# Four loads and one sum moved in a two-block transformer kernel

## The chip, the cores and the metric

The kernel runs on one core of a Trainium2 chip. The metric is device time in microseconds (us) of one launch. Three runs of the kernel before gave 2931.91, 2932.08 and 2934.31 us, a median of 2932.08 us.

## The reference

Two transformer blocks, one after the other, on 1024 tokens of width 1024, all in float32. What the change touches:

```
# block 1
u = rmsnorm(x);  z = u @ w_in;  q, k, v, pz, ga, gp = split(z)
for g in 3 head groups (dilations 1, 4, 16):
    s = q_g k_g^T / 8 + alibi_g          # bias by distance, -1e30 outside the window
    o_g, lse_g = softmax(s) v_g
a = sum over g of softmax(lse)_g * o_g
p = pool branch of pz
merged = sigmoid(u @ w_ga) * (a @ w_att_out) + sigmoid(u @ w_gp) * (p @ w_pool_out)
h = x + merged @ w_out
m = rmsnorm(h)
h = h + relu(m @ w_mlp_in)^2 @ w_mlp_out          # first feed-forward
# block 2: other attention, a recurrent unit, the same gates, and
h = h + relu(rmsnorm(h) @ w_ff1)^2 @ w_ff2        # second feed-forward
return rmsnorm(h)
```

## The kernel before

All matrices are held with channels on the 128 partitions and tokens along the free dimension; a tile `z` is 128 x 1024 float32. Every float32 product is made of three products of rounded parts (`hi*hi`, `hi*lo`, `lo*hi`), so each weight and each operand is split: ScalarE copies it to `hi`, VectorE subtracts to get `lo` (`hilo`, L476; weights in `split`, L323). A dense job (`dense`, L430) makes one 128 x 1024 result: for each of up to eight 128-row pieces of the weight it issues six matmuls of 128 x 512, and then calls `tick`.

**Order of the work.** The program is a list of jobs written in order; the schedule is the order in which instructions are issued, engine by engine, and every engine's queue is first in, first out. All data loads and stores go through SyncE's (SP's) queue. Before a job runs, the weights of the next jobs are split and those after them loaded (`run`, L390). Work that is not dense (attention steps, the merging of attention groups, sums of weights) is kept in generators in three lanes; `tick` adds the job's rate to a credit, and for every whole credit `advance` (L289) runs each lane by one step. So a step stands in the queues behind a given matmul. Buffers come from pools; a tile of a pool can be written once the last instruction that used its buffer is done, and the instruction that writes it waits in its queue for that. Pool `pz` has 36 buffers for nearly all 128 x 1024 tiles; a phase (`phase`, L269) opens a small pool of its own with five more (`t4`) and closes that of the phase before.

**Attention of block 1.** For each group, `vfn` (L1874) computes v (`v_job`, L661). For groups 1 and 2 v is stored to DRAM and read back in another order (`vd`, L705). Then `attn1` (L717) is put into lane 0. Its first step takes a buffer for the bias `alibi` and issues its load (L720 and L721); its second step issues the scores of step 0 on TensorE (L738), its third the softmax (L753 on VectorE adds the bias from SBUF to the scores in PSUM and takes the minimum of the negative; L758 on ScalarE takes exp). Later steps transpose (L768), copy (L770, L771), and multiply by v (L784). Meanwhile jobs of the pool branch run on TensorE.

**End of attention.** `combine1` (L815) merges the groups. Beside it the eight `pool_out_job` (L937) compute, copy to `po` and store it to DRAM. `att_end` (L952) drains the lanes, opens phase phC, and loads the first three chunks of the normed input (`u_load`, L959, tiles `uraw` of the phase's `t4`) from DRAM, where they were stored early in the kernel. Then `att_out_job(m)` (L963), m = 0 to 7, loads chunk m + 3, splits chunk m into `ub` on ScalarE and VectorE, issues 12 matmuls, and ScalarE copies the PSUM tile to `merged` (L976). PSUM has two tiles for such jobs.

**Feed-forward, second half.** `w_mlp_out` and `w_ff2` are applied by seven block products instead of eight (Strassen-like) over four blocks b of the hidden width. For each product i in the order 1, 2, 3, 6, 7, 5, 4 (`SEVEN_OUT`) there are four steps p, one per pair of output chunks: 12 matmuls in `seven` (L1125) into one of four PSUM banks, then `prep_step` splits the operand of the next product on steps p = 0 and p = 2 (`out_prep`, L1200: `obh`, `obl`), then the result is added (`out_ev`, L1267) to the residual `h` (`c11`, `c12`, `c21`, `c22` are its halves) and to a running sum `u` (tile `uu`). In the first block b = 0, the steps of product 1 also load the residual: step p issues two loads of 512 KB from DRAM (L1017, called at L1239) before its matmuls. For product 1 ScalarE copies the bank to `u` (L1276) and VectorE adds the bank to `c11` (L1278); product 2 adds to `c11` again by L1278. Both feed-forwards run this code.

Of the kernel before, what the change touches and what calls it, by code (L numbers as in the profile page):

```python
# [13 lines left out]
ALU = mybir.AluOpType  # L14
# [4 lines left out]
NC = D // P  # L19
# [177 lines left out]
class Kern:  # L197
# [519 lines left out]
    def attn1(self, g, src):  # L717
        nc = self.nc
        d = DIL[g]
        bias = self.z(nm="alibi")  # L720
        nc.sync.dma_start(bias, self.ins["alibi"][g])  # L721
        steps = []
        for j in range(8):
            prev = (j > 0) if g == 0 else (j % 2 == 1 if g == 1 else False)
            for hp in range(2):
                steps.append((j, hp, prev))
        n = len(steps)
        ot = {}

        def scores(t):  # L730
            j, hp, prev = steps[t]
            w = (2 if prev else 1) * P
            q, k = src["q", hp], src["k", hp]
            pss = []
            for h in range(2):
                sl = slice(64 * h, 64 * h + 64)
                ps = self.bank()
                nc.tensor.matmul(  # L738
                    ps[:, :w], q[sl, j * P:(j + 1) * P], k[sl, (j + 1) * P - w:(j + 1) * P], start=True, stop=True)
                pss.append(ps)  # L740
            return pss

        def softmax(t, pss):
            j, hp, prev = steps[t]
            w = (2 if prev else 1) * P
            if hp == 0:
                ot[j] = self.ph.tile([P, 4, 66], F32, tag="o", name="o", bufs=3)
            o = ot[j]
            s = p = self.ph.tile([P, 512], F32, tag="s", name="s", bufs=3)
            for h in range(2):  # L750
                hh = 2 * hp + h
                b1 = (hh + 1) * 256
                nc.vector.tensor_tensor_reduce(  # L753
                    out=s[:, h * w:(h + 1) * w], in0=pss[h][:, :w], in1=bias[:, b1 - w:b1],
                    scale=-1.0, scalar=BIG, op0=ALU.add, op1=ALU.min, accum_out=o[:, hh, 64:65])
            for h in range(2):
                hh = 2 * hp + h
                nc.scalar.activation(  # L758
                    p[:, h * w:(h + 1) * w], s[:, h * w:(h + 1) * w], AF.Exp,
                    bias=o[:, hh, 64:65], scale=-1.0, accum_out=o[:, hh, 65:66])  # L760
            return p

        def flip(t, p):
            nb = 2 if steps[t][2] else 1
            w = nb * P
            ps = self.bank()
            for q in range(2 * nb):
                nc.tensor.transpose(ps[:, q * P:(q + 1) * P], p[:, q * P:(q + 1) * P], self.ident())  # L768
            pt = self.ph.tile([P, 512], F32, tag="pt", name="pt", bufs=3)
            nc.scalar.activation(pt[:, :w], ps[:, :w], AF.Copy)  # L770
            nc.vector.tensor_copy(pt[:, w:2 * w], ps[:, w:2 * w])  # L771
            return pt

        def values(t, pt):
            j, hp, prev = steps[t]
            nb = 2 if prev else 1
            o = ot[j]
            ps = self.bank()
            for h in range(2):
                hh = 2 * hp + h  # L780
                for b in range(nb):
                    kt = j - nb + 1 + b
                    v0 = (kt % 4) * 256 + 64 * hh
                    nc.tensor.matmul(  # L784
                        ps[:, 64 * h:64 * h + 64], pt[:, (h * nb + b) * P:(h * nb + b + 1) * P],
                        src["v", kt // 4][:, v0:v0 + 64], start=(b == 0), stop=(b == nb - 1))
            nc.vector.tensor_copy(
                o[:, 2 * hp:2 * hp + 2, 0:64], ps[:, :P].rearrange("p (h e) -> p h e", h=2))
            if hp == 1:
                scr = self.oscr[g]  # L790
                if d == 1:
                    dst = scr[j * P:(j + 1) * P, :]
                elif d == 4:
                    dst = scr.rearrange("(i d) c -> d i c", d=4)[j // 2, (j % 2) * P:(j % 2 + 1) * P]
                else:
                    dst = scr.rearrange("(i d) c -> d i c", d=8)[j]
                nc.sync.dma_start(dst, ot.pop(j).rearrange("p h e -> p (h e)"))

        yield
        pss = scores(0)  # L800
        yield
        p, pt = {}, {}
        for t in range(n + 2):
            if t < n:
                p[t] = softmax(t, pss)
                yield
            if 0 <= t - 1 < n:
                pt[t - 1] = flip(t - 1, p.pop(t - 1))
            if t >= 2:
                values(t - 2, pt.pop(t - 2))  # L810
            if t + 1 < n:
                pss = scores(t + 1)
            yield
# [123 lines left out]
    def pool_out_job(self, un, m):  # L937
        nc = self.nc

        def fn():  # L940
            ps = self.lin(un, 0, self.pms)
            t = self.z(nm="po")
            nc.scalar.activation(t, ps, AF.Copy)
            nc.sync.dma_start(self.po[m], t)
            if m == NC - 1:
                self.pms = [None] * 6
        return fn
# [4 lines left out]
    def att_end(self):  # L952
        self.drain()
        self.phase("phC")
        self.uraw = {}
        for c in range(3):
            self.u_load(c)

    def u_load(self, c):  # L959
        self.uraw[c] = self.t4(nm="uraw")  # L960
        self.nc.sync.dma_start(self.uraw[c], self.ud[c])

    def att_out_job(self, ua, m):  # L963
# [300 lines left out]
            self.uu[p // 2] = self.z(nm="uu")  # L1264
        return self.uu[p // 2][:, (p % 2) * H:(p % 2) * H + H]

    def out_ev(self, after=None):  # L1267

        nc = self.nc
        V, G = nc.vector, nc.gpsimd  # L1270

        def ev(i, p, ps):
            u = self.half_u(i, p)
            c11, c12, c21, c22 = (half(self.h[2 * p + e], a) for e in range(2) for a in range(2))
            if i == 1:
                nc.scalar.activation(u, ps, AF.Copy)  # L1276
            if i in (1, 2):
                V.tensor_tensor(c11, ps, c11, ALU.add)  # L1278
            elif i == 3:
                V.tensor_tensor(c12, ps, c12, ALU.add)  # L1280
            elif i == 6:
                V.tensor_tensor(u, ps, u, ALU.add)  # L1282
                G.tensor_tensor(c12, c12, u, ALU.add)  # L1283
            elif i == 7:
                V.tensor_tensor(u, ps, u, ALU.add)
                G.tensor_tensor(c22, c22, u, ALU.add)
                G.tensor_tensor(c21, c21, u, ALU.add)
            elif i == 5:
                V.tensor_tensor(c12, ps, c12, ALU.add)
                V.tensor_tensor(c22, ps, c22, ALU.add)  # L1290
            else:
                V.tensor_tensor(c21, ps, c21, ALU.add)
            if after:
                after(i, p)
        return ev

    def ff(self, pr, w1, w2, gname, after):
        pr.rate = 1.0
        for i in range(N_IN0):
            un = Unit(w1, 0, NC, i * P, P)  # L1300
            pr.job([un], self.ff_in_job(un, i), 4 if i == N_IN0 - 1 else None)
        steps = []
# [15 lines left out]
        for n, i in order:  # L1318
            quad, st = pairs[n]
            extra = before_out(tail[i]) if n == nq - 1 and i in tail else None  # L1320
            un = Oper(quad, i)
# [6 lines left out]
        for b in range(N_BLK):  # L1328
            two = twos(b)
            for i in SEVEN_OUT:  # L1330
                for p in range(4):
                    un = two[i, p // 2]
                    steps.append(((un, None)[p % 2], self.block_step(Pick(un, p % 2), b, p, self.out_ev())))
        end = after == self.end_after
        for n, (un, fn) in enumerate(steps):
            ahead = 6 if end and n >= len(steps) - 4 else 4 if isinstance(un, Oper) else 3
# [7 lines left out]
        for i in SEVEN_OUT:  # L1344
            for p in range(4):
                un = two[i, p // 2]
# [494 lines left out]
    def program(self):  # L1841
# [17 lines left out]
        for g in range(3):  # L1859
# [8 lines left out]
            for c in range(2):  # L1868
                un = Unit("w_in", 0, NC, 768 + 256 * g + P * c, P)
# [4 lines left out]
            def vfn(vf=vf, g=g):  # L1874
                if g == 0:
                    self.rcols()
                    self.phase("phA")
                vf()
                self.bg[0].append(self.attn1(g, qkv[g]))
                if g == 2:  # L1880
                    self.bg[0].append(self.combine1())
# [6 lines left out]
        for half in (1, 0):  # L1888
            un = Unit("grp", 7 * half, 7, 0, P)
            pr.job([un], self.grp_job(un, half))  # L1890
        for m in range(NC):
            un = Unit("w_pool_out", 0, 6, P * m, P)
# [3 lines left out]
        for m in range(NC):  # L1896
            un = Unit("w_att_out", 0, 2, P * m, P)
            pr.job([un], self.att_out_job(un, m), 2)
        pr.job([], lambda: (self.bg[2].append(self.weight_sums(N_SUMS)), self.bg[1].append(self.lru_const())))
        for m in range(NC):  # L1900
            un = Unit("w_in", 0, NC, 3072 + P * m, P)
            pr.job([un], self.ga_job(un, m))
            un = Unit("w_in", 0, NC, 4096 + P * m, P)
            pr.job([un], self.gp_job(un, m))
        for m in range(NC):
            un = Unit("w_out", 0, NC, P * m, P)
# [41 lines left out]
        for hh in range(2):  # L1948
            pr.rate = 1.0 if hh == 0 else 1.2
            for c in range(2):  # L1950
                un = Unit("w_in_2", 0, NC, 256 * hh + P * c, P)
                pr.job([un], self.qk2_job(un, qkv2[hh], ("q", c), 0.125, 2 * hh + c))
            for c in range(2):
                un = Unit("w_in_2", 0, NC, 512 + 256 * hh + P * c, P)
# [32 lines left out]
        for m in range(NC):  # L1987
            if m == NC - 1:
                pr.job([], self.lru_end, 0)
            un = Unit("w_att_o", 0, 4, P * m, P)  # L1990
# [3 lines left out]
        for m in range(NC):  # L1994
            un = Unit("w_rec_o", 0, NC, P * m, P)
            pr.job([un], self.rec_job(un, m))
        for m in range(NC):
            un = Unit("w_out_2", 0, NC, P * m, P)
# [210 lines left out]
```

## Time and profile before

| | |
|---|---|
| median of three runs | 2932.08 us |
| the profiled execution, whole | 2933.28 us |
| its span, first to last instruction | 2931.5 us |
| TensorE busy | 2860.9 us (98%) |
| VectorE, ScalarE, GpSimd busy | 1918.1, 1166.6, 935.3 us |
| mean granted TensorE clock | 0.989 |

The 1.8 us between the profiled execution and its span lie outside the first and the last instruction. TensorE is busy nearly always, so the few stretches in which it stands, or runs at a lower granted clock (1.00 is full speed), are where the other engines and the loads show in the time. In a row of the timeline the first number is the start, the second the duration, and the bracket at the end is how long the engine had been idle and what ended that.

### The profile page before, as it was taken

Reading aid. Unit: us, or ns where it says so; the run is one execution under the profiler, and the core shown is the slowest. Engines: PE = TensorE matmul, PEld = TensorE weight load, DVE = VectorE, ACT = ScalarE, POOL = GpSimd, SP = SyncE. Lnnn points to the kernel's source line nnn. Section 1 sums busy time; section 2 is a strip of 40 time slices with the busy share of each in tenths; the row PEclk is TensorE's granted clock in tenths of the full one; section 3 lists DMA queues with packets and bytes.
Section 4 is the critical chain, followed back from the end, with each engine's and each line's share of the span. In section 5 each row is a group of like instructions: output and inputs, shape, how many; then the busy total and the mean of one; then the engine's idle time right before and its main releaser. Section 6 shows DMA issues by size and latency. Waiting matters only on the chain. (4 is left out here: it accounts for less than half of the span.)

```text
span 2931.5 us, 35187 instructions
## 1 busy us (share of the span) xinstructions
PE 2860.9 (98%) x13422; PEld 2353.4 (80%) x13422; DVE 1918.1 (65%) x2441; ACT 1166.6 (40%) x1762; POOL 935.3 (32%) x482
## 2 busy tenths in 40 slices
PE   9999999999999999999999999999999899999997
PEld 8888877888878878887878778788888788878886
DVE  6434456666765558888744336999655855569897
ACT  3322234223344444334333325565424354444344
POOL 0021102554144423334500005555144144413336
PEclk9999999999999999999999999999999999999999
DMA  4221136677233354442233222121776232264452
GB/s 162 79 69 51 69 114 221 257 275 267 80 108 115 115 212 155 157 152 86 89 122 92 95 72 69 61 79 69 281 299 223 83 118 103 106 222 158 152 167 85
DMA packets 136599, 402.34 MB, mean 137 GB/s; under 512 B 13808, under 2 KB 32368, under 8 KB 136432
## 3 DMA queue, kind: packets, MB, share of 16 engines
q1 hardware_dynamic: 136432, 400.10, 39.0%
q8 instruction: 106, 1.74, 0.2%
q14 instruction: 61, 0.50, 0.0%
HBM read 287.75 MB, written 112.30 MB: 136 GB/s over the span
## 5 line engine op out<-in xcount | busy, mean ns | idle before, releaser
L1132 PE MATMUL bk<-obl,whi 128*128 128x512 f32 x864 | 338.4, 392 | 8.6 <-DVE obl L478 8.6
L477 ACT ACTIVATE whi<-raw 128x512 fp32r<-128x512 f32 (+2 forms) x256 | 204.9, 808 | 348.3 <-PE bk L1132 234.4
L1132 PE MATMUL bk<-obh,whi 128*128 128x512 f32 x864 | 338.0, 391 | 1.6 <-DVE h L1290 1.6
L1132 PE MATMUL bk<-obh,wlo 128*128 128x512 f32 x864 | 337.8, 391 | 0.3 <-DVE wlo L478 0.3
L439 PE MATMUL mm<-uh,whi 128*128 128x512 f32 x896 | 288.0, 403 | 5.2 <-ACT uh L490 2.5
L439 PE MATMUL mm<-ul,whi 128*128 128x512 f32 x896 | 279.1, 393 | 0.3 <-DVE ul L491 0.3
L439 PE MATMUL mm<-uh,wlo 128*128 128x512 f32 x896 | 278.5, 392 | 0.3 <-DVE wlo L339 0.3
L478 DVE TENSOR_TENSOR wlo<-raw,whi 128x512 fp32r<-128x512 f32 (+2 forms) x256 | 254.5, 997 | 36.5 <-ACT whi L477 36.4
L1132 PE MATMUL bk<-tt,whi 128*128 128x512 f32 x896 | 275.8, 389 | 0.0
L378 POOL TENSOR_TENSOR wsum<-wsum 128x1024 f32<-128x1024 f32 x64 | 182.6, 2863 | 230.7 <-DMA wsum<-in_w 228.4
L339 DVE TENSOR_TENSOR wlo<-raw,whi 128x1024 fp32r<-128x1024 f32 (+3 forms) x140 | 228.3, 1636 | 34.0 <-ACT whi L338 33.9
L439 PEld LDWEIGHTS mm<-uh,whi 128*128 128x128 f32 x896 | 163.3, 190 | 64.5 <-issue 27.5
L439 PEld LDWEIGHTS mm<-ul,whi 128*128 128x128 f32 x896 | 169.5, 189 | 37.8 <-DVE ul L491 1.5
L439 PEld LDWEIGHTS mm<-uh,wlo 128*128 128x128 f32 x896 | 169.1, 189 | 37.6 <-DVE wlo L339 1.1
L1132 PEld LDWEIGHTS bk<-obl,whi 128*128 128x128 f32 x864 | 163.3, 189 | 43.8 <-DVE obl L478 9.8
L1132 PEld LDWEIGHTS bk<-tt,whi 128*128 128x128 f32 x896 | 168.2, 188 | 34.8
L1283 POOL TENSOR_TENSOR h<-h,uu 128x512 f32<-128x512 f32 x32 | 70.9, 2228 | 386.4 <-DVE uu L1282 386.4
L1132 PEld LDWEIGHTS bk<-obh,whi 128*128 128x128 f32 x864 | 163.1, 189 | 36.5 <-DVE h L1290 2.0
L1132 PEld LDWEIGHTS bk<-obh,wlo 128*128 128x128 f32 x864 | 163.3, 189 | 34.5 <-DVE wlo L478 0.8
L338 ACT ACTIVATE whi<-raw 128x1024 fp32r<-128x1024 f32 (+3 forms) x140 | 135.6, 974 | 137.3 <-PE mm L676 52.5
L1132 PE MATMUL bk<-tt,wlo 128*128 128x512 f32 x448 | 174.3, 389 | 0.0
L478 DVE TENSOR_TENSOR obl<-hraw,obh 128x1024 fp32r<-128x1024 f32 x112 | 154.6, 1381 | 13.3 <-ACT obh L477 10.2
(355 smaller groups left out, 6212.3 us busy)
## 6 DMA issues: line engine op xcount, KB each, us to landing
raw<-in_w SPq DMA_DIRECT2D x190, 512.0 KB
wsum<-in_w SPq DMA_DIRECT2D x64, 512.0 KB
sums<-wsum SPq DMA_DIRECT2D x64, 512.0 KB
hraw<-hid SPq DMA_DIRECT2D x64, 512.0 KB
raw<-sums SPq DMA_DIRECT2D x64, 512.0 KB
hid<-h SPq DMA_DIRECT2D x56, 512.0 KB
wraw<-in_w SPq DMA_DIRECT2D x28, 512.0 KB
rb<-in_rpb SPq DMA_DIRECT2D x24, 384.0 KB
```

The lines of the kernel that those rows point to most:

```text
L338: nc.scalar.activation(un.hi, un.raw, AF.Copy)
L339: nc.vector.tensor_tensor(un.lo, un.raw, f32(un.hi), ALU.subtract)
L378: G.tensor_tensor(d, x, y, f)
L439: nc.tensor.matmul(dst[a], w, half(x, a), start=(i == 0 and q == 0), stop=(i == n - 1 and q == 2),)
L477: self.nc.scalar.activation(hi, src, AF.Copy)
L478: self.nc.vector.tensor_tensor(lo, src, f32(hi), ALU.subtract)
L1132: nc.tensor.matmul(ps, w[:, k * P:(k + 1) * P], x, start=(k == 0 and q == 0), stop=(k == n - 1 and q == 2))
L1283: G.tensor_tensor(c12, c12, u, ALU.add)
```

## The change

Three edits. The bias of each attention group is loaded in `vfn` before `vf()`, that is ahead of the group's v job, and `attn1` uses that tile. The first three input chunks are loaded by the jobs `pool_out_job` m = 5, 6 and 7, before their matmuls, and all eight `uraw` tiles come from pool `pz` instead of the phase's `t4`. In block b = 0 of each feed-forward's second half, product 1 is no longer added to `c11` on VectorE; it is only copied to `u`, and after product 2 has been added to `c11`, GpSimd adds `u` to it. The loads of the residual stay where they are.

```
     def attn1(self, g, src):
-        bias = self.z(nm="alibi")
-        nc.sync.dma_start(bias, self.ins["alibi"][g])
+        bias = self.alibi
...
     def pool_out_job(self, un, m):
         def fn():
+            if m == 0:
+                self.uraw = {}
+            if m >= NC - 3:
+                self.u_load(m + 3 - NC)
             ps = self.lin(un, 0, self.pms)
...
     def att_end(self):
         self.drain()
         self.phase("phC")
-        self.uraw = {}
-        for c in range(3):
-            self.u_load(c)
     def u_load(self, c):
-        self.uraw[c] = self.t4(nm="uraw")
+        self.uraw[c] = self.z(nm="uraw")
...
-    def out_ev(self, after=None):
+    def out_ev(self, after=None, first=False):
...
             if i == 1:
                 nc.scalar.activation(u, ps, AF.Copy)
-            if i in (1, 2):
+            if i == 1 and first:
+                pass
+            elif i in (1, 2):
                 V.tensor_tensor(c11, ps, c11, ALU.add)
+                if first:
+                    G.tensor_tensor(c11, c11, u, ALU.add)
...
-    steps.append((..., self.block_step(Pick(un, p % 2), b, p, self.out_ev())))
+    steps.append((..., self.block_step(Pick(un, p % 2), b, p, self.out_ev(first=b == 0))))
...
             def vfn(vf=vf, g=g):
                 if g == 0:
                     self.rcols()
                     self.phase("phA")
+                self.alibi = self.z(nm="alibi")
+                self.nc.sync.dma_start(self.alibi, self.ins["alibi"][g])
                 vf()
```

## Rows read from the trace of the kernel before

**Rows 1.** The page, part 1: busy us, share of span, instructions.

```profile
PE 2860.9 (98%) x13422; PEld 2353.4 (80%) x13422; DVE 1918.1 (65%) x2441; ACT 1166.6 (40%) x1762; POOL 935.3 (32%) x482
```

**Rows 2.** TensorE's waits over the span: total us, times, longest.

```profile
PE bk L1132 <- DVE t L1168: 17.1, 2, 8.6
PE bk L1132 <- DVE obl L478: 8.6, 3, 3.9
PE bk L768 <- ACT s L758: 8.2, 2, 4.8
PE mm L439 <- ACT merged L976: 3.4, 2, 2.9
```

**Rows 3.** Windows: length, busy us of each engine (instructions), granted clock, DMA.

```profile
189.00:192.80 3.80, 0.45 (x3) 0.03 (x2) 0.90 (x8) 0.56 (x3) 0.00 (x0) 0.98 0.56 231
192.80:200.00 7.20, 7.20 (x19) 5.03 (x20) 3.28 (x9) 3.29 (x12) 4.33 (x4) 0.53 0.01 2
351.00:356.50 5.50, 0.70 (x4) 0.24 (x2) 0.87 (x8) 0.54 (x3) 0.00 (x0) 1.00 0.89 358
356.50:364.00 7.50, 7.49 (x24) 5.55 (x24) 2.05 (x8) 3.41 (x13) 0.00 (x0) 0.54 0.00 0
466.70:470.20 3.50, 0.61 (x3) 0.19 (x1) 0.91 (x1) 1.97 (x2) 0.00 (x0) 1.00 1.01 353
470.20:474.30 4.10, 3.55 (x14) 2.66 (x15) 2.21 (x4) 2.86 (x5) 0.00 (x0) 1.00 1.02 381
1081.40:1088.00 6.60, 2.51 (x9) 1.16 (x7) 3.18 (x4) 3.55 (x4) 0.00 (x0) 0.92 1.03 404
1088.00:1096.00 8.00, 7.97 (x23) 6.41 (x24) 5.44 (x7) 1.34 (x2) 0.00 (x0) 0.64 0.69 279
2611.30:2615.60 4.30, 0.43 (x3) 0.03 (x1) 1.82 (x2) 2.41 (x3) 0.00 (x0) 1.00 1.03 415
2615.60:2620.00 4.40, 4.40 (x12) 3.50 (x13) 1.82 (x2) 0.00 (x0) 0.00 (x0) 0.61 1.00 406
2650.00:2675.00 25.00, 25.00 (x112) 20.71 (x111) 23.77 (x26) 8.39 (x9) 19.70 (x10) 1.00 0.72 252
```

**Rows 4.** Timeline of VectorE in the attention, groups 1 and 2.

```profile
191.90 0.29 DVE L753 CUSTOM_DVE_ANT_0 s<-bk,alibi 128x128 f32<-128x128 f32 x1 [11.84 <-DMA alibi<-in_alibi]
...
349.58 1.28 DVE L931 SCALAR_TENSOR_TENSOR pml<-mm,cst,pmh 128x1024 fp32r<-128x1024 f32 x1
355.63 0.29 DVE L753 CUSTOM_DVE_ANT_0 s<-bk,alibi 128x128 f32<-128x128 f32 x1 [4.77 <-DMA alibi<-in_alibi]
```

**Rows 5.** Timeline of SP's queue in group 2.

```profile
348.25 0.81 SPq L714 DMA_DIRECT2D vd<-v  x2
349.16 0.38 SPq L321 DMA_DIRECT2D raw<-in_w  x1
349.58 0.43 SPq L721 DMA_DIRECT2D alibi<-in_alibi  x1
```

**Rows 6.** Timeline at the end of attention, SP's queue and ScalarE.

```profile
463.71 1.32 SPq L961 DMA_DIRECT2D uraw<-ud  x3
...
468.21 1.06 ACT L477 ACTIVATE ubh<-uraw 128x1024 fp32r<-128x1024 f32 x1 [4.66 <-DMA uraw<-ud]
```

**Rows 7.** Timeline of VectorE at block 0 of the second feed-forward.

```profile
2608.14 0.69 DVE L1278 TENSOR_TENSOR h<-bk,h 128x512 f32<-128x512 f32 x1 [2.10 <-ACT uu L1276]
...
2613.70 0.69 DVE L1278 TENSOR_TENSOR h<-bk,h 128x512 f32<-128x512 f32 x1 [3.73 <-DMA h<-res]
2614.30 1.22 DVE L478 TENSOR_TENSOR obl<-hraw,obh 128x1024 fp32r<-128x1024 f32 x1
2617.06 0.69 DVE L1278 TENSOR_TENSOR h<-bk,h 128x512 f32<-128x512 f32 x1 [1.54 <-DMA h<-res]
...
2620.75 0.69 DVE L1278 TENSOR_TENSOR h<-bk,h 128x512 f32<-128x512 f32 x1 [1.86 <-DMA h<-res]
...
2650.82 1.71 DVE L478 TENSOR_TENSOR obl<-hraw,obh 128x1024 fp32r<-128x1024 f32 x1
```

**Rows 8.** Source L1283, GpSimd's add to the residual: ns min/median/max.

```profile
L1283 POOL TENSOR_TENSOR h<-h,uu x32: 2201/2212/2278, 1114.9 to 2868.4; 128x512 f32<-128x512 f32 x32
```

More of the change, by code (lines that the diff above doesn't have):

```diff
@@ L1332, in ff @@
                     un = two[i, p // 2]
-                    steps.append(((un, None)[p % 2], self.block_step(Pick(un, p % 2), b, p, self.out_ev())))
+                    steps.append(((un, None)[p % 2], self.block_step(Pick(un, p % 2), b, p, self.out_ev(first=b == 0))))
         end = after == self.end_after
```

## The prediction

> **What bounds the kernel now.** I read the page's busy times first: TensorE is busy for 98% of the span, VectorE, the next, for 65% [rows 1]. A change on another engine therefore pays only where TensorE stands or runs slowly, so I took TensorE's waits next [rows 2]: few lines, each stopping it two or three times. One is L1168 (17.1 us), which the change doesn't touch. The other three are the places that it does touch: L768 behind ScalarE's exp, L439 behind ScalarE's copy to merged, L1132 behind VectorE's obl. Then I cut windows around each stop [rows 3]. In each pair of windows the first row shows how long TensorE stood (length less busy), the second how long it ran at a lower granted clock afterwards. The stops of over 3 us at 189, 351, 1084 and 2611 us are each followed by a stretch at 0.53 to 0.64, a mixture of the levels 1.2 and 2.4 GHz; the one at 467 us is not. Last I went to the timelines of VectorE, ScalarE and SP at each stop to see what began it [rows 4 to 7].
>
> The price of a stop is the standing time plus (1 - clock) times the window behind it.
>
> - Group 1's bias, 189 to 200 us: 3.80 - 0.45 = 3.35, and 0.47 x 7.20 = 3.38, together 6.7 us.
> - Group 2's bias, 351 to 364 us: 5.50 - 0.70 = 4.80, and 0.46 x 7.50 = 3.45, together 8.2 us.
> - Input chunks, 466.7 to 474.3 us: 2.89 + 0.55 = 3.4 us, the clock at 1.00 throughout.
> - Residual, first feed-forward, 1081.4 to 1096 us: 4.09 standing (a short wait and a long one), 0.08 x 6.60 = 0.53 and 0.36 x 8.00 = 2.88, together 7.5 us.
> - Residual, second feed-forward, 2611.3 to 2620 us: 3.87, and 0.39 x 4.40 = 1.72, together 5.6 us.
>
> The sum is 31.4 us, the most that the change can give back if nothing else is late.
>
> **Bias loads.** The three loads are moved, not added: three issues on SP and 1.5 MB, as before. Now VectorE's first softmax waits for the bias, 11.84 us in group 1 and 4.77 us in group 2 [rows 4]; behind it on VectorE and ScalarE everything is queued, and TensorE's transposes wait for the exp. In group 2 the load is issued at 349.58 us, behind the vd loads and a weight [rows 5], and used at 355.63: 6.0 us. Issued before the v job it passes on SP the two v stores (which wait for the end of the v job), the vd loads and the weight; the v job is 320 matmuls of 128x256, tens of us, so the load is done long before its use. It can hold SP up only by waiting for a buffer. I count the tiles in use from the code: at most 28 of 36 at group 0's v job, 27 at group 1's, 34 at group 2's, so one more fits, and the free ones were freed before the job began. Cost of the move: nothing; without that cover SP would stand until a buffer is free.
>
> What is late next? Group 1: the scores exist and VectorE is free at 180 us (its idle 11.84 us end at 191.90), TensorE needs the exp at 189: nothing. Group 2: VectorE is busy until 349.58 + 1.28 = 350.86 with L931 [rows 4]; then the softmax (0.3) and ScalarE's exp come some 0.9 us later, at about 351.8 and 352.2 for the two heads, where TensorE stands from 351.7 (0.70 us busy from 351.0 on). I leave 0.4 us there, too short for the clock to fall if the stop at 467 us, 2.9 us long with the clock at 1.00 behind it, is a guide. Next on the path is vd, read by L784 twelve matmuls (2.7 us at 112 in 25 us [rows 3]) later, near 355. Four transfers fill 351 to 356.5 us at 358 GB/s, 0.89 of the DMA engines; without the bias' 0.5 MB that work ends about 1.5 us earlier, and vd stands first in it. So 6.7 + 8.2 - 0.4 = 14.5 us.
>
> **Input chunks.** The three loads are issued at 463.71 us, behind the last po store, and ScalarE's first split waits 4.66 us for them until 468.21 [rows 6]; merged is queued behind that split on ScalarE, and with two PSUM tiles TensorE stops. Moved, each load stands on SP ahead of the po store of its own job, so chunk 0 is issued one or more jobs of 36 matmuls (8 us) earlier, and all three have landed before 462. They pass three po stores and the weight loads issued between; none of these is due within the 0.44 us that one issue takes (1.32 for three). The tiles in use there are 22 of 36 at most by my count, so taking them from the large pool costs no wait. Next late would be chunk 3 and the small weights; with the 1.5 MB out of the way both come earlier than now. ScalarE has per job a split (1.06), a copy of about the same length and a small weight split, by estimate 2.5 us against TensorE's 2.7: TensorE remains the later. 3.4 us.
>
> **Residual.** VectorE's queue in block 0 is in order: L1278 for step p = 1 waits 3.73 us for the residual until 2613.70, and obl, the operand of product 2, stands behind it and starts at 2614.30 [rows 7]; TensorE stands until 2615.6. The change removes this L1278 (four per feed-forward, 0.69 us each, eight in all) and adds to nothing that is due at that time: obl then stands only behind one weight split (1.22 us) and ScalarE's half, and is done before TensorE asks for it at 2611. The first use of the residual becomes product 2's add, four steps of 12 matmuls later. Without the stop product 2's steps end at about 2612.7, 2615.4, 2618.1 and 2620.8; the residual has landed by 2608.1, 2613.7, 2617.1 and 2620.75 now [rows 7]. The margins are 4.6, 1.7, 1.0 and 0.1 us; but the last loads are issued behind a weight load that itself waits for a VectorE split delayed by the same stall, so they should come earlier. If one is 1 or 2 us late, VectorE waits that long, with product 6's obl behind it; that is due one product later, so TensorE has some 8 us of cover. All of 7.5 + 5.6 = 13.1 us.
>
> Added are eight adds on GpSimd (four per feed-forward), 2.21 us each by its nearest row, the same shape [rows 8]. GpSimd is idle there (0.00 in the windows at 2611 and 2615 us [rows 3]), and the next writer of u is product 6, eight steps (22 us) later: hidden. What they cost VectorE: beside GpSimd's adds obl takes 1.71 us, without them 1.22 [rows 7], so 0.5 us per add, 2 us per feed-forward, against a product's 10.9 us of TensorE. VectorE's own work in product 2 is two obl, two weight splits, two operand sums (1.22 each) and four adds (0.69), 10.1 us: with 2 us more it falls 1.2 us behind and catches up later. Bounds: 0, and, if each add held VectorE for its whole length, 8 x 2.21 = 17.7 us. I take 0, near the measured side, because with GpSimd busy 19.70 of 25 us and VectorE 23.77, TensorE is full [rows 3].
>
> One rule speaks against this. The Trainium skill's page "SBUF — State Buffer" (Terms) says that VectorE and GpSimd arbitrate for one port pair that is "held for the full instruction", the loser blocking fully. The trace agrees that they disturb each other, but 19.70 + 23.77 us in 25 show that they are not exclusive as a whole.
>
> **Sum.** 14.5 + 3.4 + 13.1 = 31.0 us. The profiled execution took 2933.28 us (its span and 1.8 us outside), which leaves 2902.3; it lay 1.2 us above the median of the runs shown, so I expect a median of 2901 us.
>
> **Rivals.**
>
> 1. The residual is still late (10%). The loads are at 1.03 of the DMA share there, so they cannot come much sooner; if TensorE stops again at product 3, the 13.1 us shrink to between 0 and half: 2907 to 2914 us. Against it: obl no longer stands behind the wait when it is due.
> 2. Vd takes the bias' place (8%): L784 stops for 1 to 4 us, and where the stop is over 3 us the clock costs 3.4 more, in both groups at worst. 2904 to 2915 us. Against it: it was issued ahead of the bias.
> 3. GpSimd holds VectorE fully (3%): VectorE's 10.1 us in product 2 become 18.9 against 10.9, 8 us late in each feed-forward: 2901 + 16 = 2917 us. Against it: the window at 2650 us. It is the result by the rule of the Trainium skill's page "SBUF — State Buffer" named above.
> 4. Slower than before (5%): the buffers. The uraw tiles and the longer-lived biases change which buffer each later tile of pool pz gets. At the start of each feed-forward my count finds all 36 in use, and TensorE already stands there for 8.6 us twice [rows 2]. If a tile there now waits for a buffer that is freed later, each stop grows; from 16 us more per feed-forward on, the gain is gone: at 20 us each 2901 + 40 = 2941 us. Against it: the number of tiles in use at that place doesn't change, and all moved tiles are long free.
> 5. The loads do not come earlier, since SP reaches them late (3%): only the residual's part remains, 2919 us.
>
> The forecast itself has 71%, 2898 to 2905 us. The range must take in most of rivals 1 and 2: 2896 to 2914. A difference under 0.2% (5.9 us) can't be told from none here. Faster by more: the forecast and nearly all of rivals 1, 2, 3 and 5, 0.92; slower by more 0.04; the rest 0.04.
>
> **What would show it.** In the profile after, the waits for alibi, uraw and (on the path) res are gone; TensorE's waits keep L1168 at about 17 us and lose L768, L976 and most of obl; the windows that answer to those above show a clock of 1.00; L1278 has 56 instructions, GpSimd eight more adds. The forecast is wrong if TensorE shows a new line of waits above 3 us, or if one of the five stops is still there.

## The result and the profile after

| | before | changed |
|---|---|---|
| median, us | 2932.72 (4 runs, 2931.91 to 2934.31) | 2899.44 (4 runs, 2898.22 to 2901.12) |
| profiled execution, us | 2933.28 | 2898.60 |
| its span, us | 2931.5 | 2896.8 |
| mean granted TensorE clock | 0.989 | 0.994 |

The ratio is 0.9886, with a 95% interval of 0.9869 to 0.9903: 1.1% faster, 33.3 us between the medians. A second comparison of the same two kernels gave 0.9895 (0.9880 to 0.9910), 31.3 us (the run a1_changed below). The forecast was 2901 us.

Part 1 of the page of the changed kernel, which answers to [rows 1]:

```profile
PE 2843.8 (98%) x13422; PEld 2342.8 (81%) x13422; DVE 1911.2 (66%) x2433; ACT 1168.7 (40%) x1762; POOL 954.4 (33%) x490
```

TensorE issues the same 13,422 matmuls and is busy 17.1 us less, because fewer of them run at the lower clock. Some 12 us of that are the slow stretches behind four of the stops ([rows 3]: 3.4, 3.5, 3.4 and 1.7 us); most of the rest are slow stretches in places that the change doesn't touch, of which this execution had fewer. The other 17.6 us of the 34.7 that the span lost are standing. VectorE has eight instructions fewer, GpSimd eight more.

TensorE's waits after (total us, times, longest), which answer to [rows 2]:

```profile
PE bk L1132 <- DVE t L1168: 17.1, 2, 8.7
PE mm L1432 <- DVE h L1440: 4.3, 2, 3.2
PE bk L1729 <- ACT gt L1716: 3.7, 2, 2.4
...
PE bk L1132 <- DVE obl L478: 0.9, 1, 0.9
```

Of the four lines in [rows 2] only the one that the change doesn't touch is as it was. The wait for obl fell from 8.6 to 0.9 us, and the lines of L768 and merged are gone. The prediction named a new line above 3 us as a sign of being wrong. None is new: the lines of L1432 and L1729, in other stages, stood at 3.1 and 2.6 us before (as L1428 and L1725) and have each got a second, shorter wait, together 2.3 us. That varies between executions: in e10_load_later the second of them is 2.4 us, in e5_add_no_wait the first is 3.2.

The windows after, which answer to [rows 3] (length, busy us of PE, PEld, DVE, ACT, POOL with their instructions, granted clock, DMA share, GB/s): group 1, group 2, chunks, first and second feed-forward.

```profile
184.00:189.00 5.00, 5.00 (x25) 3.83 (x24) 0.51 (x4) 0.88 (x4) 0.00 (x0) 1.00 0.96 307
189.00:200.00 11.00, 11.00 (x55) 8.37 (x54) 4.51 (x13) 3.71 (x11) 8.45 (x8) 1.00 0.06 24
338.00:345.00 7.00, 7.00 (x34) 4.84 (x32) 6.85 (x15) 2.98 (x7) 0.00 (x0) 1.00 0.54 181
345.00:357.00 12.00, 11.94 (x68) 9.53 (x68) 5.86 (x20) 7.37 (x25) 0.00 (x0) 1.00 0.27 104
448.00:462.00 14.00, 14.00 (x63) 11.60 (x62) 8.34 (x11) 12.12 (x17) 0.00 (x0) 1.00 0.85 280
1060.00:1068.00 8.00, 8.00 (x37) 6.64 (x36) 6.47 (x7) 5.74 (x7) 0.14 (x1) 1.00 1.01 387
1068.00:1080.00 12.00, 12.00 (x55) 9.93 (x54) 11.97 (x10) 4.95 (x6) 8.63 (x4) 1.00 0.79 314
2578.00:2585.00 7.00, 7.00 (x32) 5.79 (x32) 5.43 (x5) 4.93 (x8) 0.00 (x0) 1.00 1.00 381
2585.00:2600.00 15.00, 15.00 (x68) 12.43 (x67) 14.97 (x15) 7.08 (x8) 8.48 (x4) 1.00 0.70 279
```

TensorE is full in all five places, and its clock is 1.00 throughout: both halves of each stop's price are gone. The DMA engines are as busy around the residual as before (1.00 and 1.01); nobody on the path waits for them.

To see where the time went, I set each matmul of one trace beside the same matmul of the other (both have 13,422, in one order) and took the difference of their starts. The saving grows in steps, here taken over the whole of each place:

| place | forecast, us | step between the traces, us |
|---|---|---|
| group 1's bias | 6.7 | 3.51 + 3.17 = 6.7 |
| group 2's bias | 8.2 - 0.4 = 7.8 | 7.8 |
| input chunks | 3.4 | 3.20 + 0.82 = 4.0 |
| residual, first feed-forward | 7.5 | 7.6 |
| residual, second feed-forward | 5.6 | 5.8 |
| sum | 31.0 | 31.8 |

In group 1 the two summands are the standing and the slow stretch behind it. The other 2.8 us of this pair of executions come from places that the change doesn't touch, gains and losses of up to 2 us each. Among them are two stretches at half clock, worth 1.7 us each: the one after 1401 us in the trace of before is 6.8 us long and 3.4 in the trace after, and the one after 1882 us, 3.4 us long, is missing after. Neither belongs to the change: in a1_changed the second is there, and in e5_add_no_wait the first is 6.8 us long.

### The profile page after: what moved, and what is told of

The parts are those of the page before. It is cut to its first block, busy times and chain, and to the rows that moved or that the text cites. A ratio compares the mean times of both kernels' runs of the same rounds, so it can differ in the third digit from the quotient of the medians.

```text
span 2896.8 us, 35194 instructions
## 1 busy us (share of the span) xinstructions
PE 2843.8 (98%) x13422; PEld 2342.8 (81%) x13422; DVE 1911.2 (66%) x2433; ACT 1168.7 (40%) x1762; POOL 954.4 (33%) x490
## 4 chain that ended last, share of the span: by engine, by line
PE 84%; DVE 9%; ACT 3%; issue 2%; DMA 1%; SPq 0%; POOL 0%; DVEq 0%; ACTq 0%; POOLq 0%
PE bk L1132 37%; PE mm L439 33%; PE bk L439 2%; PE bk L1558 2%; PE mm L674 1%; PE bk L1592 1%; PE mm L676 1%; PE mm L675 1%; DVE wlo L339 1%; PE bk L783 1%; PE bk L1729 1%; PE bk L737 1%; PE bk L1579 1%; PE mm L650 1%; DVE tt L478 1%
## 5 line engine op out<-in xcount | busy, mean ns | idle before, releaser
L478 DVE TENSOR_TENSOR wlo<-raw,whi 128x512 fp32r<-128x512 f32 (+2 forms) x256 | 256.7, 1006 | 37.1 <-ACT whi L477 37.1
L478 DVE TENSOR_TENSOR obl<-hraw,obh 128x1024 fp32r<-128x1024 f32 x112 | 156.6, 1398 | 16.0 <-ACT obh L477 12.8
```

The costliest lines, as they stand in the source:

```text
L478: self.nc.vector.tensor_tensor(lo, src, f32(hi), ALU.subtract)
```

## The experiments

Three things were open: which part gives what, whether the loads' places or something beside them is the cause, and whether the residual's gain is the wait or the work. "Before" and "changed" name the kernel that is edited.

**The three parts alone.** Kernel e1_bias is before with the edit of the biases only, e2_chunks with the chunks' only, e3_resid with the residual's only (their diffs are the three parts of the diff above).

> The kernel before with the bias loads moved alone. Theory (five stops, each priced by its standing time and the slow clock behind it): both stops before L768 go, the other three stay; 14.5 us less than the kernel before, ratio 0.9951. Rival (vd takes the place of the bias): TensorE waits at L784 instead, 4 to 9 us less.

> The kernel before with the input chunks loaded earlier alone, from the large pool. Theory: the waits for merged (L976) go, 3.4 to 4.0 us less, ratio 0.9987. Rival (the clock behind the stop counts too, as at the other stops): more than 5 us. Rival (buffers shifted): slower, with longer waits for L1168 at the feed-forwards.

> The kernel before with the first output product kept out of the residual alone. Theory: the waits for obl at the start of both second halves go, 13.1 us less, ratio 0.9955. Rival (the residual is still late): 0 to 7 us less, with a wait of TensorE at product 3 or 6.

Before beside them: 2932.20 us.

| kernel | median, us | ratio, 95% interval | steps beside before's trace, us |
|---|---|---|---|
| e1_bias | 2919.99 | 0.9955 (0.9943 to 0.9968) | 3.51 + 3.17 + 7.75 = 14.4 |
| e2_chunks | 2929.39 | 0.9989 (0.9980 to 0.9997) | 3.20 + 0.82 = 4.0 |
| e3_resid | 2921.03 | 0.9956 (0.9943 to 0.9970) | 7.63 + 5.75 = 13.4 |

The product of the ratios is 0.9900, beside 0.9886 and 0.9895 for the whole: within the intervals the parts add up, and none needs another. Each takes away its own line of waits and leaves the others. TensorE's waits of e1_bias, e2_chunks and e3_resid in turn (line numbers shift with the edits):

```profile
PE bk L1131 <- DVE t L1167: 17.0, 2, 8.6
PE bk L1131 <- DVE obl L478: 9.1, 3, 4.1
PE mm L439 <- ACT merged L975: 3.2, 2, 2.9
```

```profile
PE bk L1133 <- DVE t L1169: 17.2, 2, 8.6
PE bk L1133 <- DVE obl L478: 9.2, 3, 4.2
PE bk L768 <- ACT s L758: 7.6, 2, 5.0
```

```profile
PE bk L1132 <- DVE t L1168: 17.1, 2, 8.6
PE bk L768 <- ACT s L758: 8.3, 2, 4.8
PE mm L439 <- ACT merged L976: 3.2, 2, 2.9
```

In e1_bias no wait for vd has taken the bias' place, so rival 2 is out. The wait on L1168, at the place where all 36 buffers are in use, is the same in all of them and in the changed kernel, so the moved tiles cost no wait there: rival 4 is out.

**Does the place in SP's queue decide for the bias?** Kernel e8_bias_behind is before with the bias loaded earlier, but behind the v job's stores and vd's loads on SP instead of ahead of them (and vf() where the v job is issued).

```diff
                     self.phase("phA")
                 vf()
+                self.alibi = self.z(nm="alibi")
+                self.nc.sync.dma_start(self.alibi, self.ins["alibi"][g])
```

> The kernel before with the bias load taken out of the lane's first step, but issued after the v job, directly behind the vd loads. Theory (the load is late because it stands behind the v store and the vd loads in SP's queue): issued at nearly the same time, 0 to 2 us less than the kernel before. Rival (the step of the lane in which it is issued made it late): most of the 14.5 us is gained.

Measured: 2928.64 us, ratio 0.9992 (0.9983 to 1.0002), beside 0.9955 for the same load a few lines earlier. SP's queue of e8_bias_behind in group 1:

```profile
181.37 2.20 SPq L712 DMA_DIRECT2D vd<-v  x4
183.61 0.47 SPq L1879 DMA_DIRECT2D alibi<-in_alibi  x1
```

And VectorE there:

```profile
189.72 0.29 DVE L752 CUSTOM_DVE_ANT_0 s<-bk,alibi 128x128 f32<-128x128 f32 x1 [10.05 <-DMA alibi<-in_alibi]
```

TensorE still waits 5.5 us for the exp (8.2 before [rows 2]). The load has passed one weight load on SP (in group 2 the one in [rows 5]): in group 1 it is issued 5.0 us behind the last v store in place of 5.5, and VectorE waits 10.05 us in place of 11.84. In this execution that gave back 4.7 us in group 1, where the first stop, now 1.6 us, had no slow clock behind it, and 0.9 us in group 2. Places that the edit doesn't touch took 2.9 us of it back (the last section has one of them). Over all runs the ratio is worth 2.3 us, with an interval that reaches past none, where e1_bias gained 13.2.

The load is early in the program and late in the queue: the stores ahead of it wait for the end of the v job. The larger part of the gain is its place ahead of these; passing the weight load may account for some of the rest.

**Pool or place for the chunks?** The change also gives the three tiles to another pool. Kernel e4_pool_only does that alone:

```diff
-        self.uraw[c] = self.t4(nm="uraw")
+        self.uraw[c] = self.z(nm="uraw")
```

> The kernel before with the input chunks taken from the large pool but still loaded where they were. Theory (the load is late because it stands behind the last po store in SP's queue): same time as the kernel before, within 0.5 us, and the stop before L439 stays at 2.9 us. Rival (the load is late because the small pool's buffers are freed late): the load is issued earlier and most of the 3.4 us is gained by the pool alone.

Measured: 2931.13 us, ratio 0.9996 (0.9987 to 1.0005). ScalarE's first split, the row that answers to [rows 6]:

```profile
466.03 1.06 ACT L477 ACTIVATE ubh<-uraw 128x1024 fp32r<-128x1024 f32 x1 [4.65 <-DMA uraw<-ud]
```

It waits 4.65 us where it waited 4.66. The pool alone gives nothing that can be told; the gain is the earlier issue's.

**The residual: the wait or the work?** The change takes a wait and an add of 0.69 us from VectorE's queue together. Kernel e5_add_no_wait is the changed kernel with as much VectorE work put back at the same point, without the residual; e6_wait_no_add puts back the wait alone, as a copy of 128x1 that reads the residual.

```diff
             if i == 1 and first:
-                pass
+                V.tensor_copy(self.z(nm="junk")[:, :H], ps)        # e5
+                V.tensor_copy(self.gg[:, 0:1], c11[:, 0:1])        # e6
```

> The changed kernel with one more instruction of VectorE in each step of product 1 of block 0: a copy of the PSUM bank (128 x 512, as large as the sum that was removed) to a tile that nobody reads. It does not read the residual. Theory (the wait for the residual's load was the cost, not VectorE's time): as the changed kernel, within 1 us, obl's waits stay gone. Rival (VectorE was too full, and the change relieved it by four sums): part of the two stops comes back, 3 to 13 us more.

> The changed kernel with a copy of one column of the residual (128 x 1) by VectorE in each step of product 1 of block 0; the result is overwritten before it is used. It takes next to no time, but waits for the residual's load where the removed sum waited. Theory: both stops before L1132 come back whole, with the slow clock behind them, 11 to 13 us more than the changed kernel. Rival (VectorE's load): no more than 1 us.

> The changed kernel once more, as the measure for the three runs beside it. The three parts alone gave ratios of 0.9955, 0.9989 and 0.9956 to the kernel before, together 0.9900. Theory (the parts don't touch each other): 0.9900, 2903 us, within 0.001. Rival (one part opens something for another): below 0.989.

Measured, the three on one chip with before (2932.61 us):

| kernel | median, us | ratio, 95% interval |
|---|---|---|
| a1_changed | 2901.30 | 0.9895 (0.9880 to 0.9910) |
| e5_add_no_wait | 2900.88 | 0.9892 (0.9878 to 0.9905) |
| e6_wait_no_add | 2913.43 | 0.9935 (0.9922 to 0.9947) |

VectorE of e6_wait_no_add in the second feed-forward, and then a line of its TensorE waits:

```profile
2594.57 0.15 DVE L1278 COPY gg<-h 128x1 f32<-128x1 f32 x1 [5.59 <-DMA h<-res]
2594.68 1.23 DVE L478 TENSOR_TENSOR obl<-hraw,obh 128x1024 fp32r<-128x1024 f32 x1
```

```profile
PE bk L1132 <- DVE obl L478: 9.1, 3, 4.2
```

Eight copies of 0.15 us cost 12.1 us, nearly all of the residual's 13: the copy stands 5.59 us for the load, and obl stands behind it. Eight copies of a whole bank that wait for no load cost nothing. The wait is the cause, and the work is free here.

**How much room has the residual now?** The prediction gave margins of 4.6, 1.7, 1.0 and 0.1 us. Kernel e10_load_later is the changed kernel with each pair of residual loads one step (12 matmuls) later.

```diff
-            if (b, i) == (0, 1):
-                for m in (2 * p, 2 * p + 1):
+            q = p - 1 if (b, i) == (0, 1) else 3 if (b, i, p) == (0, 2, 0) else -1
+            if q >= 0:
+                for m in (2 * q, 2 * q + 1):
                     self.h_load(m, self.res)
```

> The changed kernel with the residual loaded one step (2.7 us) later: the pair of chunks of step p is loaded in step p + 1, the last one in product 2's first step. Theory (a sum that waits is covered, since the next obl is due a product later): VectorE waits for the load at product 2, TensorE does not; as the changed kernel, within 1 us. Rival (the residual is only just in time): TensorE stops again at product 3 or 6, 5 to 13 us more.

Measured: 2900.50 us, ratio 0.9891 (0.9877 to 0.9904), no change. TensorE's wait for obl is 0.9 us, as in the changed kernel, and VectorE doesn't wait for the residual either, where it was expected to: the second of product 2's four sums has no idle time before it.

```profile
2587.42 0.68 DVE L1284 TENSOR_TENSOR h<-bk,h 128x512 f32<-128x512 f32 x1
```

But the loads are not a whole step later where it counts. SP's last residual loads in the second feed-forward, in the changed kernel and then in e10_load_later, whose matmuls there are 0.5 us later:

```profile
2580.43 2.78 SPq L1017 DMA_DIRECT2D h<-res  x2
```

```profile
2581.12 2.48 SPq L1017 DMA_DIRECT2D h<-res  x4
```

SP reaches the last load at 2582.9 us in the changed kernel and at 2583.2 us in e10_load_later. The table sets the landing of the four loads that product 2's sums read (from the semaphore events of the traces; the same reading puts each 0.1 us ahead of the sum that waited for it in before) against the end of the step and the start of the sum.

| ahead of, us (p = 0 to 3) | forecast | changed | e10_load_later |
|---|---|---|---|
| the end of the step's matmuls | 4.6, 1.7, 1.0, 0.1 | 4.8, 1.4, 1.6, 0.6 | 1.2, 1.0, 0.05, 0.2 |
| the start of VectorE's sum | | 6.2, 1.7, 3.7, 1.7 | 2.5, 1.4, 2.1, 1.3 |

So the forecast margins were about right. The loads stayed in time because, beside the matmuls, they landed only 3.6, 0.3, 1.6 and 0.4 us later, with the DMA engines full there (1.00 in the window at 2578 us), and because VectorE, behind by then, starts its sums later than the steps end. The run doesn't show that the loads could land a step later, or that TensorE would be covered if VectorE did wait. Rival 1 is ruled out by the changed kernel itself, in which nothing on the path waits for the residual.

**GpSimd's sums.** Kernel e7_vector_sum is the changed kernel with the eight added sums on VectorE, e9_double_sum with GpSimd doing each of them twice (once into a spare tile).

```diff
-                    G.tensor_tensor(c11, c11, u, ALU.add)
+                    V.tensor_tensor(c11, c11, u, ALU.add)                       # e7
```

```diff
+                    G.tensor_tensor(self.z(nm="junk")[:, :H], c11, u, ALU.add)  # e9
                     G.tensor_tensor(c11, c11, u, ALU.add)
```

> The changed kernel with the eight added sums (u into c11 at product 2) on VectorE instead of GpSimd. Theory (VectorE has room at product 2 and falls behind by no more than a product): as the changed kernel, within 1 us, ratio to the kernel before 0.989. Rival (VectorE is full there, and the sum had to be on GpSimd): TensorE waits for obl at products 3 or 6, 3 to 10 us more.

> The changed kernel with each of the eight added sums on GpSimd done twice, the first time into a tile that nobody reads: 2.2 us more of GpSimd per step of product 2, about 4.4 of each 2.7 us step. Theory (GpSimd is off the path and costs VectorE 0.5 us per sum): as the changed kernel, within 1 us. Rival (each sum of GpSimd holds VectorE for its whole length): 8 times 2.2 us more on VectorE, 8 to 18 us more.

Measured, beside before's 2931.5 us: e7_vector_sum 2902.04 us, ratio 0.9903 (0.9887 to 0.9920); e9_double_sum 2899.64 us, 0.9897 (0.9882 to 0.9911). Both intervals hold the changed kernel's 0.9895. The same window of e7_vector_sum and of e9_double_sum:

```profile
2580.00:2605.00 25.00, 25.00 (x112) 20.71 (x111) 22.90 (x26) 11.85 (x14) 0.00 (x0) 1.00 0.75 292
```

```profile
2580.00:2605.00 25.00, 25.00 (x112) 20.72 (x111) 21.73 (x18) 15.37 (x18) 13.44 (x7) 1.00 0.82 306
```

TensorE is full in both: neither four sums more on VectorE nor twice the work on GpSimd reaches the path. That rules out rival 3's 16 us; the last section has why VectorE is held so little.

## Why the prediction was right

**The method.** Five stops were priced from windows as standing plus slow clock, and each came back within 0.6 us of its price. The steps are taken beside the same execution from which the prices were read, so that the clock's part agrees tests little; what is tested is that the stops go and that nothing takes their place. The one price that was clearly off is the chunks': 3.4 us forecast, 4.0 measured twice, by the changed kernel and by e2_chunks. Both of its waits lie inside the windows; it is the standing, read as length less busy, that comes out short. TensorE at the first wait, in the trace of before:

```profile
466.70 0.61 PE L439 MATMUL mm<-ath,wlo 128*128 128x512 f32 x2
470.23 0.73 PE L439 MATMUL mm<-ath,whi 128*128 128x512 f32 x2 [2.91 <-ACT merged L976]
```

In a full stretch a pair like the first is shown as 0.61 us busy, but the next pair starts 0.46 us after it. So by the starts TensorE stood 3.07 us and not 2.91, and the pair behind the stop takes 0.73 us, 0.11 more. That is nearly 0.3 us a stop, and the chunks had two. The other stops have the same excess, but there the slow part came out shorter than priced (group 1: 3.17 us, priced 3.38), which offsets it.

**Biases.** VectorE in groups 1 and 2 after, the rows that answer to [rows 4]:

```profile
180.26 0.29 DVE L752 CUSTOM_DVE_ANT_0 s<-bk,alibi 128x128 f32<-128x128 f32 x1 [0.37 <-PE bk L737]
...
342.73 1.28 DVE L930 SCALAR_TENSOR_TENSOR pml<-mm,cst,pmh 128x1024 fp32r<-128x1024 f32 x1
343.92 0.29 DVE L752 CUSTOM_DVE_ANT_0 s<-bk,alibi 128x128 f32<-128x128 f32 x1
```

The first softmax of group 1 waits for the scores alone, at the 180 us that the prediction gave. In group 2 it now stands behind L930, as forecast, and TensorE's transposes run at its pace for a moment. TensorE there:

```profile
344.80 0.72 PE L767 MATMUL bk<-cst,s 128*128 128x128 f32 x2
```

The two transposes start 0.1 us late and take 0.72 us where the next pair takes 0.38: the 0.4 us that the prediction left, with the clock at 1.00 behind it. One number of this part was wrong without effect: a v job has 192 matmuls of 128x256, not 320 (that is one source line's count over the whole kernel). It still takes some 23 us or more, and group 2's load is issued at 312 us, 31 us ahead of its use.

**Chunks.** SP's queue after, the rows that answer to [rows 6], then ScalarE:

```profile
424.91 0.66 SPq L961 DMA_DIRECT2D uraw<-ud  x1
...
442.27 0.55 SPq L961 DMA_DIRECT2D uraw<-ud  x1
448.82 0.32 SPq L947 DMA_DIRECT2D po<-po  x1
```

```profile
449.30 1.05 ACT L477 ACTIVATE ubh<-uraw 128x1024 fp32r<-128x1024 f32 x1
450.48 1.03 ACT L976 ACTIVATE merged<-mm 128x1024 f32<-128x1024 f32 x1
```

The last of the three is issued 7 us ahead of the first split, ahead of the po store that it had followed. The split has no idle time before it, and merged no longer stands behind a wait. TensorE is full in the window at 448 us, so nothing that the loads pass on SP became late for it.

**Residual.** VectorE at block 0 of the second feed-forward, the rows that answer to [rows 7]:

```profile
2579.00 1.23 DVE L478 TENSOR_TENSOR obl<-hraw,obh 128x1024 fp32r<-128x1024 f32 x1 [0.21 <-ACT obh L477]
...
2585.18 0.68 DVE L1280 TENSOR_TENSOR h<-bk,h 128x512 f32<-128x512 f32 x1
...
2587.51 1.72 DVE L478 TENSOR_TENSOR obl<-hraw,obh 128x1024 fp32r<-128x1024 f32 x1
2589.26 2.20 DVE L1212 TENSOR_TENSOR hraw<-hraw 128x1024 f32<-128x1024 f32 x1
...
2593.72 1.71 DVE L478 TENSOR_TENSOR obl<-hraw,obh 128x1024 fp32r<-128x1024 f32 x1
2595.35 2.31 DVE L1214 TENSOR_TENSOR hraw<-hraw 128x1024 f32<-128x1024 f32 x1
```

Obl waits for ScalarE's half alone and starts at 2579.00, before product 2. The first sum of product 2 finds its residual there. Two sizes of this part were off without moving the time:

- The margins. They were read from the trace of before, in which SP's last residual loads stand behind a weight load that the stall itself had held up. The prediction said that these should come earlier and gave no number: it is 0.6 us for the last two (1.0 and 0.1 became 1.6 and 0.6). What it left out is that VectorE, being behind, would not use them at once.
- What GpSimd's sums cost VectorE. The prediction had 0.5 us per add and 2 us per feed-forward from obl alone. Obl was right (1.72 in place of 1.22), but the operand sums at L1212 and L1214 grow by 1.0 and 1.1 us: 2 x 0.5 + 2.1 = 3.1 us. The eight sums themselves have the length of [rows 8], with a median of 2.21 us.

VectorE is busy 14.97 of 15 us in the last window of the second feed-forward, so it does fall behind, as the prediction said; TensorE doesn't notice. The Trainium skill's page "SBUF — State Buffer" (Terms) has the shared port pair held for the full instruction, with the loser blocking fully. The trace agrees for VectorE's instructions with both inputs in SBUF: one that starts while a sum of GpSimd runs takes longer by about what is left of that sum, 0.5 to 1.1 us here (the last section has the rows). The prediction's argument against it, 19.70 + 23.77 us busy in 25, doesn't decide: the time for which an instruction is held counts as busy, as obl's 1.72 us show. Rival 3 failed for another reason. VectorE was held for 3.1 us per feed-forward and not for 8.8, since its sums from PSUM are not held and an instruction that starts first is not either, and what it lost was covered; e9_double_sum shows that twice as many sums cost the kernel nothing.

**The median.** The forecast was 2901 us, from 31.0 us off the profiled execution. The two comparisons gave 33.3 and 31.3 us between the medians. The difference between these lies within their intervals, and the stretch after 1401 us shows what can make it: untouched places run slowly for 3.4 or 6.8 us from one execution to the next. That the median came within 2 us is partly luck of this kind; the five places gave 31.8 us.

**The rivals.** Rivals 1 to 4 are ruled out as said above. Rival 5, loads that do not come earlier, is refuted by SP's rows; e8_bias_behind is what it would have looked like for the bias.

## What to carry to other kernels

Price a stop of TensorE as its standing time, by the starts of the matmuls around it, plus the slow stretch behind it, each from a window that reaches to where the clock is 1.00 and the engine full again; here five such prices gave a sum of 31.0 us where 31.8 came back. The slow stretch is that of one execution; in another it can be longer, shorter or missing. A load's time of issue is set by what stands before it in its in-order queue, not by its line in the program: look for the store ahead of it that waits for something. A wait for a load on an in-order engine costs what stands behind it, so move the first use of the loaded tile behind the work that TensorE needs next; 0.15 us of work that waits cost here nearly as much as 0.69 us that waits, and 0.68 us that didn't wait cost nothing.

## What the runs showed of the hardware

**The clock after a stop is not the same each time.** In e2_chunks the stop in group 1, which that kernel leaves in place, was 2.67 us long, and the clock stayed at 1.00 behind it. TensorE of e2_chunks, then its window:

```profile
191.78 0.71 PE L768 MATMUL bk<-cst,s 128*128 128x128 f32 x2 [2.67 <-ACT s L758]
```

```profile
188.00:196.00 8.00, 5.27 (x24) 3.56 (x24) 3.85 (x14) 2.76 (x10) 1.40 (x2) 1.00 0.38 151
```

In the trace of before, TensorE stood 3.35 us at the same place and 7.2 us at 0.53 followed [rows 3]. In e3_resid and e4_pool_only the slow stretch there was 3.4 us long in place of 6.8. So the clock's part of this stop's price, 3.4 us in the forecast, was 0, 1.7 or 3.4 us in different executions.

The length of a stop alone doesn't tell which. The stop at the chunks, which the prediction took as a guide to what is too short, is 2.9 us long in before and in e8_bias_behind. In before the clock stayed at 1.00 behind it [rows 3]; in e8_bias_behind it fell to half for 6.8 us. Its windows there, up to the fall and after it:

```profile
459.00:463.20 4.20, 2.09 (x10) 1.39 (x8) 0.13 (x1) 1.22 (x2) 0.00 (x0) 1.00 0.99 327
463.20:470.00 6.80, 6.00 (x14) 4.74 (x15) 4.38 (x5) 4.75 (x7) 0.00 (x0) 0.50 0.99 366
```

**GpSimd beside VectorE.** Sums on VectorE that read a PSUM bank keep their 0.68 us beside GpSimd's sums. For an instruction with both inputs in SBUF it matters which came first. A sum of GpSimd in e9_double_sum, then VectorE beside it:

```profile
2591.32 2.15 POOL L1282 TENSOR_TENSOR junk<-h,uu 128x512 f32<-128x512 f32 x1 [12.12 <-DVE h L1280]
```

```profile
2591.11 1.21 DVE L478 TENSOR_TENSOR wlo<-raw,whi 128x1024 fp32r<-128x1024 f32 x1
...
2592.84 1.72 DVE L478 TENSOR_TENSOR obl<-hraw,obh 128x1024 fp32r<-128x1024 f32 x1
```

The split of a weight starts 0.2 us before GpSimd's sum and keeps its 1.21 us. Obl starts with 0.63 us of that sum left and takes 0.50 us more than its 1.22. It is so in the whole trace of the changed kernel. Of VectorE's 128x1024 instructions at L478, L1210, L1212 and L1214, 32 start ahead of a GpSimd sum that falls into them and take 1.21 to 1.23 us. Another 80 start while one runs and take longer by what is left of it less 0.13 us, for rests of up to 2.3 us; a rest shorter than that costs nothing.
